# Slots and banks of a hybrid decoder layer handed out as its list scheduler reckoned, by recording the program twice

## The chip, the cores and the metric

One core of one Trainium2 chip runs the whole program. The metric is the device time of one execution in microseconds (us), lower is better. The core has five engines with an instruction queue each: TensorE (PE, matrix products), VectorE (DVE), ScalarE (ACT), GpSimd (POOL), and SyncE (SP), which here only issues DMA transfers. Instructions of one queue start in their order; between queues, semaphores hold an instruction back until its operands and its destination are ready.

## The reference: what is computed

One inference step of one decoder layer, float32, for a prompt of 2048 tokens and a decode group of 8 sequences with one token each, which share the weights. D_MODEL is 1024.

```python
y, conv_buf, sc_buf, s = parallel_mixer(rms_norm(x, norm_mix), ...)   # conv module beside gated DeltaNet, one output projection
x = x + y
x = x + memory_attend(rms_norm(x, norm_mem_q), mem_k, mem_v, w_mq, w_mo)   # 4 heads of 256 into 256 memory tokens
x = x + swiglu(rms_norm(x, norm_ffn), w_gate, w_up, w_down)               # D_FF 2816
```

The mixer projects the normalised input once. One half of the columns goes through a gated linear unit, a depthwise convolution of width 31, a layer norm and SiLU; the other half is a gated DeltaNet (4 heads of 128, chunks of 64, a recurrent 128x128 state). The memory keys and values come from 256 memory tokens. Outputs are the final norms, the conv and delta states, and the memory keys and values.

## The kernel before, in words

The prompt is worked in four blocks of 512 tokens (NB = 4, TB = 512), activations transposed: 128 channels on the partitions, tokens along the free dimension. Blocks go through the mixer in pairs, then output projection, attention and feed-forward block by block. The decode tokens' work is mixed in between. Weights arrive as 128x512 tiles called raw, are split by ScalarE into a rounded part (`w<-raw`) and by VectorE or GpSimd into the remainder (`w<-raw,w`), and TensorE multiplies with both. The feed-forward products and some others are cut further into partial products (fx, fy, fz, dx, dy, dz in the profile), which need sums of weight tiles; those sums are stored in DRAM once (`sums<-w`, `sums<-raw`) and loaded again (`w<-sums`, `raw<-sums`).

The program isn't issued in the order in which it is written. Everything is first recorded on a tape (class `Tape`): each operation with its engine, outputs, inputs and a reckoned cost (`Tape.cost`, lines 189 to 221). `Tape.order` (lines 316 to 522) is a list scheduler: it keeps a reckoned clock for each engine, always takes the engine that can start first, and takes from the operations that are ready there the one with the lowest key. `Tape.issue` then issues the operations in that order to the framework, which adds the semaphores. As every operation has the line of the call in `issue`, the profile shows L530 throughout, and groups are told apart by the names of their tiles.

Tiles live in slots. A pool has for each tag a number of slots of one size; a tile of that tag takes a slot and gives it back after its last reader. The tags that carry most of the work are: `raw` (11 slots, loaded weights), `w` (6 slots, split weights), `t2` (28 slots of 520 floats, nearly all intermediate values, among them the profile's jn, pr, kt, qb, vtd, acc, sqj, lnx), `act` (22 slots, the matmuls' activations) and, in PSUM, `mm` and `s` (three banks each) and `o` and `cv` (one bank each). An operation that begins a tile can't start before the last reader of its slot's tile before has ended, on whatever engine that is.

`Tape.order` reckons with this. For each tag it keeps a heap `free` of the times at which slots come free (line 345). An operation that begins a tile isn't taken while the lowest entry lies in its future (lines 446 and 447); when it is taken, the lowest entry is popped (line 471). When a tile's last operation is placed, its reckoned end goes back into the heap: the end of the operation plus 160 ns, or for a DMA plus 930 ns (lines 514 to 517). A DMA's end is reckoned as its issue plus 1100 ns, or the end of the transfer before if that is later, plus its size at 295 bytes per ns (lines 207 and 498); a GpSimd `tensor_tensor` as 150 ns plus 2.15 ns per element (line 221), a VectorE reduction as 68 ns plus 1.042 ns per element.

What `order` does not say is which slot it was. `TapePool.tile` (lines 550 to 557) asks the framework for a tile of the tag with its number of slots, and the framework picks the slot itself, from what it knows of the issued order.

Of the kernel before, what the change touches and what calls it, by code (L numbers as in the profile page):

```python
# [8 lines left out]
F32 = mybir.dt.float32  # L9
# [71 lines left out]
class Clock:  # L81


    def __init__(self):
        self.at = {"pe": 0.0, "act": 0.0, "dve": 0.0, "pool": 0.0, "sp": 0.0, "dma": 0.0}
        self.ready, self.used = {}, {}
        self.table = None
        self.ring, self.nbank = {}, {"mm": 3, "s": 3, "o": 1, "cv": 1}
        self.held = set()
# [65 lines left out]
class Tape:  # L155
# [8 lines left out]
        "dma": dict(pe=930, dve=950, act=910, pool=985, sp=930),  # L164
    }

    def __init__(self):
        self.ops, self.tag_of, self.bufs, self.psum, self.flex = [], {}, {}, set(), True
        self.real, self.other, self.given, self.follow = {}, {}, {}, set()

    def pool(self, pool, bufs, psum=False):
        return TapePool(self, pool, bufs, psum)
# [143 lines left out]
    def order(self):  # L316
# [15 lines left out]
        line, at, live = {}, {}, {}  # L332
# [9 lines left out]
                heappush(held, last[t])  # L342
                live[tag].append(len(held))
        key = self.keys(succs, line, first, tiles)
        free = {tag: [0.0] * self.bufs[tag] for tag in line}
        head = dict.fromkeys(line, 0)
        early = {tag: set() for tag in line}
        parked = {tag: [] for tag in line}
# [25 lines left out]
        start, end, ends = [0.0] * N, [0.0] * N, {}  # L374
# [8 lines left out]
        def cost(n, e):  # L383
            return self.ops[n][7] if e == self.ops[n][0] else self.other[n][2]
# [17 lines left out]
        done = []  # L402
        while len(done) < N:
            best = None
            for e in engines:
                if avail[e]:
                    t = clock[e]
                elif future[e]:
                    t = max(clock[e], future[e][0][0])
                else:  # L410
                    continue
                if best is None or t < best[0]:
                    best = t, e
            assert best is not None, "order"
            t, e = best
            fu, av = future[e], avail[e]
            while fu and fu[0][0] <= t:
                _, k, n = heappop(fu)
                heappush(av, (k, n))
            skipped = []  # L420
            load = taken(t) if e == "pool" else 0.0
            busy = e != "pool" or load > BACKLOG
            n = None
            while av:
                k, n = heappop(av)
                if gone[n]:
                    n = None
                    continue
                if not busy and n in self.other:
                    load += cost(n, "dve")[0]  # L430
                    busy = load > BACKLOG
                    n = None
                    continue
                at_ = bank_at(n, e)
                if at_ > t:
                    ready[n] = at_
                    heappush(fu, (ready[n], key[n], n))
                    n = None
                    continue
                new = [x for x in tiles[n] if x not in given]  # L440
                stop = None
                for x in new:
                    tag = self.tag_of[x]
                    if not may(x) or not free[tag]:
                        stop = tag, None
                    elif free[tag][0] > t:
                        stop = tag, free[tag][0]
                if stop is None:
                    if e == "dve" and cost(n, e)[1] and port_at > t + 150 and not skipped:

                        other = [(k2, m) for k2, m in av if not gone[m] and not cost(m, e)[1] and all(x in given for x in tiles[m]) and bank_at(m, e) <= t]
                        if other:
                            skipped.append((k, n))
                            k, n = min(other)
                            av.remove((k, n))
                            heapify(av)
                            new = []
                    break
                if stop[1] is None:
                    parked[stop[0]].append((e, n))  # L460
                else:
                    ready[n] = stop[1]
                    heappush(fu, (ready[n], key[n], n))
                n = None
            for x in skipped:
                heappush(av, x)
            if n is None:
                continue
            for x in new:
                tag = self.tag_of[x]  # L470
                heappop(free[tag])
                given.add(x)
                if at[x] == head[tag]:
                    ts = line[tag]
                    while head[tag] < len(ts) and ts[head[tag]] in given:
                        early[tag].discard(head[tag])
                        head[tag] += 1
                else:
                    early[tag].add(at[x])
                if parked[tag]:  # L480
                    wake(tag, t)
            ns, port, tb = cost(n, e)
            gone[n] = True
            self.given[n] = e
            s = t
            if port and e in ("dve", "pool"):
                s = max(s, port_at)
                port_at = s + ns
            if tb and tb != table:
                table = tb  # L490
                ns += 1283
            if e == "pe" and s > clock[e] + 1800 and s > 5000:
                slow = s + 3400
            if e == "pe" and s < slow:
                ns *= 1.9
            if e == "sp":
                clock[e] = s + 450
                dma_at = max(dma_at, s + 1100) + ns
                fin = dma_at
            else:  # L500
                clock[e] = fin = s + ns
            start[n], end[n] = s, fin
            done.append(n)
            for x in banks[n]:
                bank[x] = e, max(fin, bank[x][1]) if x in bank and bank[x][0] == e else fin
            lat = self.LAT["dma" if e == "sp" else e]
            for m in succs[n]:
                left[m] -= 1
                ready[m] = max(ready[m], fin + (max(lat["dve"], lat["pool"]) if m in self.other else lat[self.ops[m][0]]))
                if not left[m]:  # L510
                    push(m)
            for x in tiles[n]:
                uses[x] -= 1
                ends[x] = max(ends.get(x, 0.0), fin + (930 if e == "sp" else 160))
                if not uses[x]:
                    tag = self.tag_of[x]
                    heappush(free[tag], ends[x])
                    early[tag].discard(at[x])
                    if parked[tag]:
                        wake(tag, ends[x])  # L520
        self.start, self.end = start, end
        return done

    def issue(self, tc):
        with tc.manual_schedule():
            for n in self.order():
                eng, _, fn, args, kw, *_ = self.ops[n]
                if self.given[n] != eng:
                    fn = self.other[n][1]
                fn(*args, **kw)  # L530

# [14 lines left out]
class TapePool:  # L546
# [1 line left out]
        self.tape, self.real, self.bufs, self.psum = tape, pool, bufs, psum  # L548

    def tile(self, shape, dt, tag, name, bufs=None):  # L550
        t = self.real.tile(shape, dt, tag=tag, name=name) if bufs is None else self.real.tile(shape, dt, tag=tag, name=name, bufs=bufs)
        tp = self.tape
        key = (id(self), tag)
        tp.tag_of[t.name] = key
        tp.bufs[key] = bufs or self.bufs
        if self.psum:
            tp.psum.add(t.name)
        return t
# [91 lines left out]


@with_exitstack
def hybrid_step(ctx: ExitStack, tc: tile.TileContext, i: dict, o: list):
    nc = tc.nc
    C = Clock()
    tape = Tape()
    tape.real = {"dve": nc.vector, "pool": nc.gpsimd}
    GS, PE, SP = tape.port(nc.gpsimd, "pool"), tape.port(nc.tensor, "pe"), tape.port(nc.sync, "sp")
    V, A, G = Engine(tape.port(nc.vector, "dve"), "dve", C), Engine(tape.port(nc.scalar, "act"), "act", C), Engine(GS, "pool", C)
# [140 lines left out]
    class Plan(list):  # L800


        def __init__(self):
            self.raws, self.raw_of, self.uses, self.seen = [], [], [], []
# [21 lines left out]
    plan = Plan()  # L826
# [146 lines left out]
    for pair in PAIRS:  # L973
        for st in STEPS:
            k = int(st[1])
# [1323 lines left out]
    for pair in PAIRS:  # L2299
# [3 lines left out]
        for st in STEPS:  # L2303
# [8 lines left out]
            k = int(st[1])  # L2312
# [801 lines left out]
    for b in range(NB):  # L3114
# [5 lines left out]
        elif b + 1 < NB:  # L3120
            rest()
    S.until(lambda: not S.lanes, "end")
    tape.issue(tc)


_OUTS = [
    (KC, P, SEQ), (P, KC, DEC), (4, P, CW - 1), (P, 12, SC - 1), (1, 1, H, DK, DK), (1, 1, NM, MH, MD), (1, 1, NM, MH, MD),
    (1, DEC, CW - 2, CC), (1, DEC, SC - 2, QKV), (1, DEC, H, DK, DK), (P, 4, DEC), (P, 12, DEC),
]
# [75 lines left out]
```

## Time and profile before

| what | us |
|---|---|
| median of 3 runs (2897.68 to 2903.99) | 2903.49 |
| the profiled execution's own time | 2902.07 |
| its span, first to last instruction | 2900.4 |
| PE busy | 2851.7 |
| weight loads (PEld) busy | 2574.5 |
| DVE busy | 2456.9 |
| ACT busy | 1519.2 |
| POOL busy | 816.2 |

The span is a little shorter than the time of the execution, which has the start and the end around it. Busy times are of single engines that run beside each other. In rows such as `PE sc <- ACT pr: 4.0, 2, 3.6` the waiting engine and the tile that it writes stand left of the arrow, what ended the wait right of it, then the total in us, the number of waits and the longest. In a timeline row, start and length come first, then engine, operation, output and inputs, and in brackets how long the engine was idle before it and what ended that.

### The profile page before, as it was taken

What the parts mean: (1) busy time and instruction counts of PE and PEld (TensorE: products, weight loads), DVE (VectorE), ACT (ScalarE), POOL (GpSimd) and SP (SyncE); (2) the same over time, 40 slices, a digit from 0 to 9 for tenths busy, and PEclk for the clock granted to TensorE, in tenths of its full rate; (3) what the DMA queues carried; (4) which work ended last, traced back from release to release, by engine and by line L of the source; (5) the groups of instructions that cost most, each with busy time, mean ns of one, the idle gap of its engine ahead of it and who ended that gap; (6) DMA issues with size and microseconds to landing.
All of it is one profiled execution on the core that took longest, in us unless ns stands there. A gap on an engine that the chain in (4) does not pass through costs nothing.

```text
span 2900.4 us, 55620 instructions
## 1 busy us (share of the span) xinstructions
PE 2851.7 (98%) x19240; PEld 2574.5 (89%) x19240; DVE 2456.9 (85%) x5321; ACT 1519.2 (52%) x3426; POOL 816.2 (28%) x969
## 2 busy tenths in 40 slices
PE   9999999999899999999999999999999999999998
PEld 7999878887788787899988789999889999999998
DVE  8868999999777997998989778888867888888888
ACT  7554565646765555556555454444554444444444
POOL 3211333346235015563313710000631232400000
PEclk9999999999999999999999999999999999999999
DMA  6433434778764325766677677777527666676664
GB/s 221 146 112 102 135 123 162 239 256 251 225 217 137 119 95 166 239 200 223 219 259 263 224 247 236 251 238 238 185 89 231 206 211 196 207 238 189 216 211 129
DMA packets 363034, 569.39 MB, mean 196 GB/s; under 512 B 55840, under 2 KB 158560, under 8 KB 362736
## 3 DMA queue, kind: packets, MB, share of 16 engines
q1 hardware_dynamic: 362752, 565.84, 60.9%
q8 instruction: 152, 2.49, 0.4%
q14 instruction: 130, 1.06, 0.1%
HBM read 457.77 MB, written 108.51 MB: 195 GB/s over the span
## 4 chain that ended last, share of the span: by engine, by line
PE 84%; DVE 6%; DMA 4%; ACT 2%; issue 2%; POOL 2%; SPq 0%; DVEq 0%; POOLq 0%; ACTq 0%
PE rg L530 11%; PE fy L530 11%; PE hd L530 10%; PE fz L530 8%; PE fx L530 8%; PE dx L530 5%; PE dn L530 5%; PE sc L530 5%; PE dz L530 3%; PE glub L530 2%; PE glua L530 2%; PE mkv L530 1%; PE pu L530 1%; DVE w L530 1%; PE dy L530 1%
## 5 line engine op out<-in xcount | busy, mean ns | idle before, releaser
L530 ACT ACTIVATE w<-raw 128x512 fp32r<-128x512 f32 (+1 forms) x1066 | 649.2, 619 | 818.5 <-issue 141.0
L530 DVE TENSOR_TENSOR w<-raw,w 128x512 fp32r<-128x512 f32 (+1 forms) x849 | 600.6, 711 | 154.8 <-ACT w L530 150.3
L530 PE MATMUL fy<-op,w 128*128 128x256 f32 (+1 forms) x3168 | 434.4, 283 | 5.8 <-DVE ffs L530 5.8
L530 PEld LDWEIGHTS fy<-op,w 128*128 128x128 f32 x3168 | 400.8, 189 | 9.0 <-DVE ffs L530 6.0
L530 POOL TENSOR_TENSOR w<-raw,w 128x512 fp32r<-128x512 f32 (+1 forms) x217 | 306.8, 1420 | 306.4 <-ACT w L530 202.6
L530 PE MATMUL hd<-hT,w 128*128 128x512 f32 (+2 forms) x1920 | 390.7, 356 | 2.2 <-DVE w L530 1.1
L530 DVE SCALAR_TENSOR_TENSOR cacc<-cu,cw,cacc 128x512 f32<-128x512 f32 x480 | 358.2, 746 | 6.6 <-ACT cacc L530 3.4
L530 PEld LDWEIGHTS hd<-hT,w 128*128 128x128 f32 x1920 | 305.1, 189 | 48.0 <-ACT w L530 2.0
L530 PE MATMUL fx<-op,w 128*128 128x256 f32 (+1 forms) x2112 | 296.7, 283 | 0.1
L530 PE MATMUL fz<-op,w 128*128 128x256 f32 (+1 forms) x2112 | 287.5, 283 | 2.1 <-DMA w<-sums 2.0
L530 PEld LDWEIGHTS fx<-op,w 128*128 128x128 f32 x2112 | 269.2, 188 | 6.3 <-issue 2.6
L530 PEld LDWEIGHTS fz<-op,w 128*128 128x128 f32 x2112 | 264.2, 188 | 8.4 <-DMA w<-sums 3.3
L530 PE MATMUL dx<-fo,w 128*128 128x256 f32 (+1 forms) x1344 | 199.0, 283 | 1.6 <-DVE x L530 1.6
L530 PE MATMUL sc<-w,hT 128*128 128x512 f32 x768 | 190.6, 402 | 4.0 <-ACT pr L530 4.0
L530 PE MATMUL rg<-pT,w 128*128 128x512 f32 x768 | 191.1, 401 | 3.0 <-ACT pT L530 1.4
L530 PE MATMUL dn<-ff,w 128*128 128x512 f32 (+2 forms) x960 | 191.9, 353 | 0.4 <-DVE ffs L530 0.4
L530 PE MATMUL rg<-catS,w 128*128 128x512 f32 (+2 forms) x960 | 191.5, 354 | 0.0
L530 PEld LDWEIGHTS dx<-fo,w 128*128 128x128 f32 x1344 | 174.9, 188 | 5.3 <-DVE x L530 3.8
L530 PEld LDWEIGHTS rg<-catS,w 128*128 128x128 f32 x960 | 155.9, 189 | 24.1
L530 PEld LDWEIGHTS sc<-w,hT 128*128 128x128 f32 x768 | 142.0, 189 | 37.4 <-ACT pr L530 6.0
L530 PEld LDWEIGHTS rg<-pT,w 128*128 128x128 f32 x768 | 141.9, 189 | 36.5 <-ACT pr L530 2.2
L530 PEld LDWEIGHTS dn<-ff,w 128*128 128x128 f32 x960 | 151.9, 189 | 23.1 <-DVE x L530 0.9
(435 smaller groups left out, 4898.0 us busy)
## 6 DMA issues: line engine op xcount, KB each, us to landing
w<-sums SPq DMA_DIRECT2D x222, 512.0 KB, 4.5
raw<-in_w_gate_dram SPq DMA_DIRECT2D x192, 256.0 KB, 3.5
sums<-w SPq DMA_DIRECT2D x66, 512.0 KB, 4.0
raw<-in_w_up_dram SPq DMA_DIRECT2D x118, 256.0 KB, 3.6
raw<-in_w_down_dram SPq DMA_DIRECT2D x224, 128.0 KB, 3.0
raw<-in_w_in_dram SPq DMA_DIRECT2D x96, 256.0 KB, 3.1
raw<-sums SPq DMA_DIRECT2D x74, 256.0 KB, 3.2
raw<-wk SPq DMA_DIRECT2D x64, 256.0 KB, 2.8
```

Source lines behind the costliest of these rows:

```text
L530: fn(*args, **kw)
```

## The change

The program is recorded twice. The first recording runs `order` and returns the tape, which keeps the order (`done`), the engine given to each operation (`given`) and, new, for each tile the number of the slot that `order` popped for it (`place`). The heap's entries become pairs of time and slot number for this. The second recording builds the same program on a fresh context with the first tape as its plan; its `TapePool.tile` looks up the number that the plan holds for the tile that was created at the same place of the recording, and asks the framework for a tile of a tag of its own for that slot (`mm_0`, `mm_1`, `t2_17`) with one slot. So the framework has no choice left. It issues the operations in the plan's order on the plan's engines; both are what `order` gave before, since the pairs are popped by their time. Tags with one slot, DRAM tiles among them, stay as they are.

```diff
-        free = {tag: [0.0] * self.bufs[tag] for tag in line}
+        free = {tag: [(0.0, k) for k in range(self.bufs[tag])] for tag in line}
...
-                    elif free[tag][0] > t:
-                        stop = tag, free[tag][0]
+                    elif free[tag][0][0] > t:
+                        stop = tag, free[tag][0][0]
...
-                heappop(free[tag])
+                self.place[x] = heappop(free[tag])[1]
...
-                    heappush(free[tag], ends[x])
+                    heappush(free[tag], (ends[x], self.place[x]))
...
-        self.start, self.end = start, end
+        self.start, self.end, self.done = start, end, done
...
     def issue(self, tc):
         with tc.manual_schedule():
-            for n in self.order():
+            for n in self.plan.done:
                 eng, _, fn, args, kw, *_ = self.ops[n]
-                if self.given[n] != eng:
+                if self.plan.given[n] != eng:
                     fn = self.other[n][1]
                 fn(*args, **kw)
...
     def tile(self, shape, dt, tag, name, bufs=None):
-        t = self.real.tile(shape, dt, tag=tag, name=name) if bufs is None else self.real.tile(shape, dt, tag=tag, name=name, bufs=bufs)
+        plan = self.tape.plan
+        if plan and (bufs or self.bufs) > 1:
+            t = self.real.tile(shape, dt, tag=f"{tag}_{plan.place[plan.names[len(self.tape.names)]]}", name=name, bufs=1)
+        elif bufs is None:
+            t = self.real.tile(shape, dt, tag=tag, name=name)
+        else:
+            t = self.real.tile(shape, dt, tag=tag, name=name, bufs=bufs)
         tp = self.tape
+        tp.names.append(t.name)
...
-def hybrid_step(ctx: ExitStack, tc: tile.TileContext, i: dict, o: list):
+def hybrid_step(ctx: ExitStack, tc: tile.TileContext, i: dict, o: list, slots=None):
...
-    tape = Tape()
+    tape = Tape(slots)
...
+    if slots is None:
+        tape.order()
+        return tape
     tape.issue(tc)
...
+    nc, ins, outs = program()
+    plan = hybrid_step(_tile.TileContext(nc).__enter__(), ins, outs)
+    nc, ins, outs = program()
     with _tile.TileContext(nc) as tc:
-        hybrid_step(tc, ins, outs)
+        hybrid_step(tc, ins, outs, plan)
```

More of the change, by code (lines that the diff above doesn't have):

```diff
@@ L165, with __init__ @@
     }
-    def __init__(self):
+    def __init__(self, plan=None):
         self.ops, self.tag_of, self.bufs, self.psum, self.flex = [], {}, {}, set(), True
         self.real, self.other, self.given, self.follow = {}, {}, {}, set()
+        self.place, self.names, self.plan = {}, [], plan
     def pool(self, pool, bufs, psum=False):
@@ L3192, with program @@
     from concourse.bass_utils import run_bass_kernel_spmd as _run
-    nc = _bacc.Bacc("TRN2", target_bir_lowering=False, num_devices=1, dynamic_dma_scratch_size=1024)
-    arrays, ins, outs = {}, {}, []
-    for name, a in lay_out(inputs).items():
-        arrays[f"in_{name}_dram"] = a
-        ins[name] = nc.dram_tensor(f"in_{name}_dram", a.shape, _mybir.dt.from_np(a.dtype), kind="ExternalInput").ap()
-    for k, shape in enumerate(_OUTS):
-        outs.append(nc.dram_tensor(f"out_{k}_dram", shape, F32, kind="ExternalOutput").ap())
+    arrays = {f"in_{name}_dram": a for name, a in lay_out(inputs).items()}
+    def program():
+        nc = _bacc.Bacc("TRN2", target_bir_lowering=False, num_devices=1, dynamic_dma_scratch_size=1024)
+        ins, outs = {}, []
+        for name, a in arrays.items():
+            ins[name[3:-5]] = nc.dram_tensor(name, a.shape, _mybir.dt.from_np(a.dtype), kind="ExternalInput").ap()
+        for k, shape in enumerate(_OUTS):
+            outs.append(nc.dram_tensor(f"out_{k}_dram", shape, F32, kind="ExternalOutput").ap())
+        return nc, ins, outs
+    nc, ins, outs = program()
+    plan = hybrid_step(_tile.TileContext(nc).__enter__(), ins, outs)
+    nc, ins, outs = program()
     with _tile.TileContext(nc) as tc:
-        hybrid_step(tc, ins, outs)
+        hybrid_step(tc, ins, outs, plan)
     r = _run(nc, [arrays], core_ids=[0])
```

## The prediction

> **What bounds the kernel now.** I began with the page's totals.
>
> ```profile
> span 2900.4 us, 55620 instructions
> ...
> PE 2851.7 (98%) x19240; PEld 2574.5 (89%) x19240; DVE 2456.9 (85%) x5321; ACT 1519.2 (52%) x3426; POOL 816.2 (28%) x969
> ...
> PE 84%; DVE 6%; DMA 4%; ACT 2%; issue 2%; POOL 2%; SPq 0%; DVEq 0%; POOLq 0%; ACTq 0%
> ```
>
> TensorE is busy for all but 2900.4 - 2851.7 = 48.7 us, and the chain that ended last (third line) runs through it for 84%. The change adds and removes no matmul, and it issues each queue in the same order as before; it only decides which slot a tile lies in. So it can win back no more than part of these 48.7 us, and what a lower clock costs behind them. Next I read what TensorE waited for, in the view of waits of that engine.
>
> ```profile
> PE fy L530 <- DVE ffs L530: 5.8, 1, 5.8
> PE sc L530 <- ACT pr L530: 4.0, 2, 3.6
> PE wk L530 <- ACT jn L530: 3.0, 2, 1.7
> PE pu L530 <- DMA Tm<-zt: 2.0, 1, 2.0
> PE fz L530 <- DMA w<-sums: 2.0, 4, 0.9
> ...
> PE rg L530 <- ACT pT L530: 1.4, 2, 1.1
> PE po L530 <- ACT osc L530: 1.4, 1, 1.4
> ...
> PE hd L530 <- ACT w L530: 1.1, 1, 1.1
> ```
>
> Few waits are long, and each happens once or twice. The longest, 5.8 us, is of a matmul whose second half goes into a bank from which VectorE still has to read the first half; VectorE came late to that read because of its own queue. No slot is part of it. In the next two the bank of the matmul is waited for, and ScalarE, which empties it, is late. Whether ScalarE was late because of a slot is the question, so I looked at the timeline and the chain around both.
>
> ```profile
> 1643.12 7.96 POOL L530 TENSOR_TENSOR kt<-kt,qb 128x512 f32<-128x512 f32 x6
> ...
> 1646.14 0.68 DVE L530 TENSOR_REDUCE scs<-kt 128x2 f32<-128x512 f32 x1
> ...
> 1649.89 0.56 ACT L530 ACTIVATE pr<-sc,mx,rs 128x256 f32<-128x256 f32 x1 [4.24 <-POOL kt L530]
> ...
> 1651.15 1.97 PE L530 MATMUL sc<-w,hT 128*128 128x512 f32 x6 [3.55 <-ACT pr L530]
> ```
>
> Here is the mechanism that the change is about. `pr` reads sc, mx and rs. It reads nothing that GpSimd wrote, yet ScalarE stood idle for 4.24 us until a GpSimd product ended. So the new pr tile was given the t2 slot of a qb tile that GpSimd was still reading. At 1646.14 + 0.68 = 1646.82 VectorE had finished its last read of a kt tile, three microseconds sooner; the slot of that one went to another tile. GpSimd's product had its place earlier in the order, and ended later.
>
> ```profile
> 754.93 5.70 DMA wk<-jn
> ...
> 760.66 0.70 ACT jn L530
> ...
> 761.40 0.79 PE wk L530 x2
> ```
>
> The chain around the other wait shows a slot too: jn is written from PSUM, and had to wait for the DMA that still stored the jn tile before it in that slot.
>
> **The change, part by part.** The forecast is made against the profiled execution, 2902.07 us with a span of 2900.4; the median of the three runs, 2903.49, lies 1.42 above it.
>
> *Slots that GpSimd reads last (pr).* The scheduler reckons a GpSimd product over 512 elements at 150 + 512 x 2.15 = 1251 ns, and 160 ns until the slot is free: 1.41 us. It reckons VectorE's reduction at 68 + 512 x 1.042 = 602 ns, free after 0.76 us. With both started within 0.65 us of each other VectorE's slot is free first by its reckoning, and pr gets that one. I take it so, as GpSimd's slot was the oldest by order alone. Then pr begins at about 1646.84, its two activations and their accumulator reads take about 1.2 us, and the matmul that began at 1651.15 begins at 1648.1. But the pr tile after it is in the same position.
>
> ```profile
> 1649.82 1.26 POOL L530 TENSOR_TENSOR kt<-kt,qb 128x512 f32<-128x512 f32 x1
> ...
> 1651.11 0.56 ACT L530 ACTIVATE pr<-sc,mx,rs 128x256 f32<-128x256 f32 x1
> ```
>
> GpSimd ended the next product at 1651.08, and the next pr began at 1651.11. If that tile keeps its slot, its bank comes free at about 1651.11 + 1.2 = 1652.3 as before; TensorE has done the six matmuls of the row of 1651.15 by 1648.1 + 1.97 = 1650.1 and waits there for 2.2 us. Before, it had done them at 1653.1; now it goes on at 1652.3: 0.8 us won of a wait of 3.55. That is what is late next. The ends are 0 (pr keeps its slot) and 3.0 us (all of them get other slots).
>
> The clock comes on top. The windows view gives the granted clock around both waits.
>
> ```profile
> 759.50:761.40 1.90, 0.21 (x3) 0.02 (x2) 1.32 (x3) 0.74 (x2) 0.00 (x0) 1.00 0.01 2
> 761.40:764.90 3.50, 3.50 (x16) 3.50 (x17) 0.00 (x0) 1.90 (x6) 0.00 (x0) 0.51 0.77 263
> ...
> 1652.30:1655.80 3.50, 3.50 (x11) 2.58 (x10) 3.21 (x10) 1.11 (x5) 0.00 (x0) 0.51 0.03 5
> ```
>
> The first number behind the window's length is TensorE's busy time, the third from the end the clock. After each of the two idle stretches the clock is halved for 3.5 us, which costs half of that, 1.7 us. With pr's wait broken into pieces of 0.5 and 2.2 us the halving may stay away or not; a stretch with 0.21 us busy in 1.90 was enough at 761, so I count half, 0.85 us. Sum of this part: 0.8 + 0.85, about 1.7 us won; bounds 0 and 3.0 + 1.7 = 4.7.
>
> [...]
>
> pr's old slot now goes to another taker, most likely a load of vtd, which was issued in those microseconds. SP then waits for GpSimd, up to 3.0 us, with the loads queued behind it. I cost that at nothing, as TensorE waits for weight loads so rarely (below); without that cover it is the 3.0 us.
>
> *Slots that a DMA reads last (jn, stored w).* The store of jn took 5.70 us. Reckoned it is 1.10 + 262144 / 295 = 0.89 + 0.93 = 2.92 us. Both the framework and the plan took or take this slot for free when it isn't; I see no reason for another choice and cost it at 0. Its bounds are the waits of 3.0 us with the halved clock, 1.7, won; and on the other side new waits of this kind. The nearest rows for those:
>
> ```profile
> sums<-w SPq DMA_DIRECT2D x66, 512.0 KB, 4.0
> ACT w L530 <- DMA sums<-w: 12.7, 9, 4.7
> L530 ACT ACTIVATE w<-raw 128x512 fp32r<-128x512 f32 (+1 forms) x1066 | 649.2, 619 | 818.5 <-issue 141.0
> ```
>
> A stored w tile takes 4.0 us and is reckoned at the same 2.92, so its slot seems free 1.1 us too soon; nine of these 66 already hold ScalarE up, by 1.4 us each. ScalarE has room (818.5 us idle before `w<-raw`), and of that only 1.1 us reached TensorE (`PE hd <- ACT w`). Upper end: 5 us lost, as if one wait like pr's came back with its clock.
>
> *Slots of raw tiles and SP's queue.* A raw tile is last read by ScalarE, VectorE or GpSimd.
>
> ```profile
> SPq L530 <- POOL w L530: 253.4, 147, 11.3
> L530 DVE TENSOR_TENSOR w<-raw,w 128x512 fp32r<-128x512 f32 (+1 forms) x849 | 600.6, 711 | 154.8 <-ACT w L530 150.3
> L530 POOL TENSOR_TENSOR w<-raw,w 128x512 fp32r<-128x512 f32 (+1 forms) x217 | 306.8, 1420 | 306.4 <-ACT w L530 202.6
> ```
>
> GpSimd's product takes 1.42 us, VectorE's 0.71. Where GpSimd's slot was taken first only because it was placed first, the load behind it starts up to 0.7 us sooner, 147 times at most. TensorE waited for DMAs for 2.0 + 2.0 us in its view, and no raw load is among them, so the bounds are 4.0 us won and nothing. I take 0.5, near the low end, since eleven raw slots lie between load and use.
>
> *PSUM banks.* TensorE writes the banks in order, and with three in turn the one freed longest ago is the same by the order of issue and by reckoned ends, unless two readers overtake each other. `rg <- pT` and `po <- osc` (1.4 us each) are such waits; o has one bank and no choice. I take 0, with 1.4 us either way. Further waits on other semaphores than before are a few instructions each and lie beside TensorE's work.
>
> Sum: 1.7 + 0 + 0.5 + 0 = 2.2 us won. 2902.07 - 2.2 = 2899.9 for the profiled execution, and 2903.49 - 2.2 = 2901.3 for the median.
>
> **Rivals.**
>
> *Nothing changes.* The framework may choose almost as the plan does, so that only a handful of tiles lie elsewhere, pr among those that don't move. For it: the list above holds only one TensorE wait that another choice would clearly have spared. It gives 2903.5. Chance 0.2, within "same".
>
> *Faster.* Every slot wait falls: pr 4.7, the two waits for jn and the clock 3.0 + 1.7 = 4.7, DMA 4.0, one bank 1.4, together 14.8: 2888.7; half of it, 7.4 us, gives 2896.1. For it: one trace shows pr and jn by their names, and smaller ones may hide behind other releasers. Against: jn's slot was reckoned free, and TensorE takes back little where the next tile is late as well. Chance 0.25.
>
> *Slower: GpSimd later than reckoned.* The plan trusts GpSimd to free a slot 1.41 us after the start of the product. At 1643 it had six products queued back to back (7.96 us), and the last ended eight microseconds after the first began. Where GpSimd lags behind its reckoned start by more than the slack of the slot, the plan hands ScalarE or VectorE the later slot with confidence. Each such place on the way to a bank costs what pr's did, 3.55 + 1.7 = 5.25 us. It decides from two new places on: 2 x 5.25 - 2.2 = 8.3 us lost, 2911.8. Against: GpSimd is busy for only 28%, and by order alone it was preferred even more. Chance 0.13.
>
> **How the numbers follow.** What a measurement can tell from no change is about 0.2%, 5.8 us. The forecast of 2.2 us won has 0.42 and lies within it, as does "nothing changes" with 0.2: 0.62 for the same. Faster has 0.25, slower 0.13. The likeliest case alone spans 2898 to 2904. The range for all cases reaches down to 2893, which takes in the nearer half of the faster rival, and up to 2909, short of the slower one at its two places but with a single one.
>
> **What would show it.** Right: TensorE's count stays at 19240, its idle time falls to about 46 us, `ACT pr <- POOL kt` of 4.24 us near 1650 shrinks to about 1, a wait of sc on pr of some 2 us remains, SP waits less than 253.4 us for POOL w, and wk's waits for jn stay at 3.0. Wrong: an unmoved pr (nothing changes); both jn and pr gone and an idle time under 40 us (faster); new waits of TensorE above 3 us behind ScalarE with a GpSimd releaser, each followed by half a clock (slower).

## The result, and the profile after

The kernel after the change takes 2893.48 us (median of 20 executions, 2890.08 to 2901.0), the kernel before beside it 2901.62 (20 executions, 2895.35 to 2906.7). The ratio is 0.9977, 95% interval 0.9969 to 0.9985: 6.7 us faster, 4.4 to 9.0. Two more comparisons (e6 and e11 below) gave 9.9 and 8.7 us. The forecast was 2.2 us and "the same" within 0.2%; the ratio lies just beyond that bound, and the time inside the range of 2893 to 2909, by half a microsecond. One execution of e9 below took 3068.63 us, far above all others, and is left out of its median and ratio.

The two profiled executions show less of it, 2902.07 us against 2899.17. The latter is one of the slowest of its 20 executions; part of why executions of one kernel differ by several us is in the last section. First the totals of the page after the change.

```profile
span 2897.4 us, 55611 instructions
...
PE 2849.6 (98%) x19240; PEld 2574.3 (89%) x19240; DVE 2460.6 (85%) x5321; ACT 1520.3 (52%) x3426; POOL 813.4 (28%) x969
```

TensorE's count is the same. Its idle time went from 48.7 us to 2897.4 - 2849.6 = 47.8. So busy and idle totals hardly tell the kernels apart. What does is the view of TensorE's waits (after the change; line 531 stands where 530 stood before).

```profile
PE fy L531 <- DVE ffs L531: 5.8, 1, 5.8
PE fz L531 <- DMA w<-sums: 2.3, 4, 1.1
PE wk L531 <- ACT jn L531: 2.1, 3, 1.3
PE hd L531 <- DVE w L531: 2.1, 1, 2.1
...
PE vp L531 <- ACT jn L531: 1.9, 3, 0.9
...
PE sc L531 <- ACT pr L531: 1.1, 1, 1.1
```

`sc <- pr` fell from 4.0 us in two waits to 1.1 in one. The waits for jn changed their form (wk 3.0 to 2.1, vp 0.6 to 1.9), not their sum (3.6 and 4.0). The timeline around pr, after the change:

```profile
1644.76 8.05 POOL L531 TENSOR_TENSOR kt<-kt,qb 128x512 f32<-128x512 f32 x6
1645.99 1.26 DVE L531 TENSOR_REDUCE scs<-kt 128x2 f32<-128x512 f32 x2
1646.70 0.56 ACT L531 ACTIVATE pr<-sc,mx,rs 128x256 f32<-128x256 f32 x1 [1.97 <-DVE scs L531]
...
1647.95 3.45 PE L531 MATMUL sc<-w,hT 128*128 128x512 f32 x13 [1.07 <-ACT pr L531]
...
1648.49 0.57 ACT L531 ACTIVATE pr<-sc,mx,rs 128x256 f32<-128x256 f32 x1 [0.58 <-DVE scs L531]
...
1651.10 0.57 ACT L531 ACTIVATE pr<-sc,mx,rs 128x256 f32<-128x256 f32 x1 [1.40 <-DVE scs L531]
```

GpSimd's six products are as long as before (8.05 us, 7.96 before), but none of these pr waits for them: all three are released by VectorE's reductions. The slot of every tile in the two programs says the same: pr_3565, pr_3566 and pr_3567 (the three activations with a wait) each had a qb tile's slot, which GpSimd reads, and now have a kt tile's, which VectorE reads. The row at 1649.89 in the prediction is the second of the three, pr_3566. The first, in the timeline of before:

```profile
1644.45 0.56 ACT L530 ACTIVATE pr<-sc,mx,rs 128x256 f32<-128x256 f32 x1 [1.36 <-POOL kt L530]
...
1645.70 1.89 PE L530 MATMUL sc<-w,hT 128*128 128x512 f32 x7 [0.45 <-ACT pr L530]
```

So the wait of 1.07 us that is left after the change stands at pr_3565, where it was 0.45 before: there the new slot came free later than the old one. The wait of 3.55 us at pr_3566 is gone, and at pr_3567 TensorE doesn't wait. The windows view has the clock of the stretch that was at 0.51 before:

```profile
1652.30:1655.80 3.50, 3.50 (x18) 2.83 (x17) 3.50 (x8) 2.98 (x7) 2.03 (x3) 1.00 0.02 5
```

18 matmuls instead of 11 in the same 3.5 us, at the full clock.

There is a second place, which the longest waits of the list don't show. Timeline of before, then of after:

```profile
516.46 0.72 ACT L530 ACTIVATE acc<-raw,scw 128x512 f32<-128x512 f32 x1 [1.59 <-PE pu L530]
...
517.20 0.55 ACT L530 ACTIVATE u<-pu 64x128 f32<-64x128 f32 x2
...
517.81 0.49 PE L530 MATMUL pch<-S,kT 128*128 128x128 f32 x2 [0.64 <-ACT u L530]
```

```profile
515.50 0.73 ACT L531 ACTIVATE acc<-raw,scw 128x512 f32<-128x512 f32 x1 [1.06 <-DMA q<-acc]
...
517.09 0.56 ACT L531 ACTIVATE u<-pu 64x128 f32<-64x128 f32 x2 [0.86 <-PE pu L531]
```

The tile acc_1028 had the slot of lt_753, which TensorE's pu matmul still had to read: ScalarE, which makes acc, waited for TensorE, and `u`, queued behind acc, then held TensorE up. Now it has the slot of acc_1015, which a DMA was storing, and the store landed first. The same run of instructions, from one `po` matmul to one `hd` matmul, in the windows view of before and of after:

```profile
512.66:524.89 12.23, 11.23 (x61) 8.70 (x60) 10.74 (x23) 6.01 (x16) 4.35 (x6) 1.00 0.59 190
```

```profile
513.30:523.98 10.68, 10.68 (x62) 8.81 (x60) 9.48 (x21) 4.83 (x13) 3.53 (x5) 1.00 0.51 165
```

12.23 us became 10.68, and TensorE's 1.00 us without work is gone.

Two more of TensorE's waits are smaller still. Timeline of before, then of after:

```profile
480.24 0.63 PE L530 MATMUL pu<-W,u 128*128 128x64 f32 x4 [0.82 <-DVE zd L530]
...
891.57 0.66 PE L530 MATMUL pvv<-ident,vT 128*128 128x128 f32 x4 [0.33 <-DVE tbm L530]
```

```profile
480.91 0.63 PE L531 MATMUL pu<-W,u 128*128 128x64 f32 x4
...
893.56 0.60 PE L531 MATMUL pvv<-ident,vT 128*128 128x128 f32 x4
```

The matmuls are the same and the waits are gone. For pvv the slots name the reason: in its bank lay a dnc tile that VectorE still had to read (into tbm), and now lies a pu tile that ScalarE reads sooner. For pu the tile in its bank is the same as before, and VectorE has read it by the time TensorE gets there; which moved slot does that isn't traced.

In all, the order on every engine is the same, and of the 3889 tiles of the tags t2, raw, w and s that have a tile before them in their slot, 363 lie behind another one than before (234 of t2, 80 raw, 29 s, 20 w); none of mm and act does.

### The profile page after: what moved, and what is told of

Read it like the earlier page. It is cut to its first block, busy times and chain, and to the rows that moved or that the text cites. A ratio compares the mean times of both kernels' runs of the same rounds, so it can differ in the third digit from the quotient of the medians.

```text
span 2897.4 us, 55611 instructions
## 1 busy us (share of the span) xinstructions
PE 2849.6 (98%) x19240; PEld 2574.3 (89%) x19240; DVE 2460.6 (85%) x5321; ACT 1520.3 (52%) x3426; POOL 813.4 (28%) x969
## 4 chain that ended last, share of the span: by engine, by line
PE 85%; DVE 6%; DMA 4%; ACT 2%; issue 2%; POOL 1%; SPq 0%; DVEq 0%; ACTq 0%; POOLq 0%
PE rg L531 12%; PE fy L531 11%; PE hd L531 11%; PE fx L531 7%; PE fz L531 7%; PE dn L531 6%; PE sc L531 5%; PE dx L531 5%; PE glub L531 3%; PE dz L531 3%; PE glua L531 3%; DMA w<-sums 2%; PE pu L531 1%; DVE w L531 1%; PE pch L531 1%
## 5 line engine op out<-in xcount | busy, mean ns | idle before, releaser
L531 PEld LDWEIGHTS hd<-hT,w 128*128 128x128 f32 x1920 | 306.1, 190 | 48.7 <-DVE w L531 2.6
```

## The experiments

The first theory was that the gain is made at pr, with the clock behind it; e2 made it **theory 1** of the later runs: it is made at two places, pr and acc. **Rivals:** it is the 230 other t2 tiles, or the raw, w and PSUM slots with SP's queue, or the naming of slots by itself. Every kernel was compared with the kernel before on the same chip; us are the ratio's distance from 1 times the median of before. The slots of a kernel are changed by a table of slot numbers or by `trade(x, y)`: from tile x on, the slot of x and the slot of y are exchanged in the plan, for all later tiles.

**e1, pr alone.** The slots of before by table, and

```diff
+        for x, y in [('pr_3565', 'kt_3592'), ('pr_3566', 'kt_3599'), ('pr_3567', 'kt_3608')]:
+            tape.trade(x, y)
```

> The slots of before, written out as a table, and only three pr tiles (and the tiles that trade places with them) moved to the slots that they have after the change. Theory A (one place): the change won its time at the pr tiles near 1650 us, where the two profiles differ by 4 to 5 us (TensorE's waits of 3.55 and 0.45 us and a halved clock worth 1.7 us). Then this kernel takes 4 to 5 us less than before, about 2897, and most of what the change won (6.7 us by the ratio 0.9977). Theory B (many places): the 363 tiles of 3889 that lie elsewhere win a little each, and pr is one of them by accident of this one profile; then this kernel is within 2 us of before.

Measured: 2896.78 us against 2901.12, ratio 0.9984 (0.9974 to 0.9993), 4.6 us faster (2.0 to 7.5). Its timeline has pr as in the kernel after:

```profile
1642.67 0.56 ACT L547 ACTIVATE pr<-sc,mx,rs 128x256 f32<-128x256 f32 x1 [1.97 <-DVE scs L547]
...
1643.92 3.45 PE L547 MATMUL sc<-w,hT 128*128 128x512 f32 x13 [1.07 <-ACT pr L547]
```

Three tiles, with their partners in the trades, give about half of what the kernel after won in its three comparisons, as theory A had it.

**e2, pr undone.** The kernel after, with the three pr tiles back behind qb tiles.

```diff
+        for x, y in [('pr_3565', 'qb_3597'), ('pr_3566', 'qb_3602'), ('pr_3567', 'qb_3607')]:
+            tape.trade(x, y)
```

> The changed kernel with only those three pr tiles put back behind the GpSimd products, the other moved tiles as changed. Theory A: 4 to 5 us slower than the changed kernel, so within 3 us of before (2 us faster than it at most), with TensorE's wait of 3.5 us for pr and the halved clock near 1652 back in the profile. Theory B: it keeps nearly all of the gain, 5 to 7 us faster than before.

Measured: 2896.35 us against 2901.12, ratio 0.9982 (0.9973 to 0.9991), still 5.2 us faster (2.6 to 7.8). The wait is back in its view (the first row), but most of the gain isn't gone with it. That pr is the whole of it was wrong; something else in the plan earns time. Its timeline led to the second place, where acc is released by the DMA as in the kernel after:

```profile
PE sc L539 <- ACT pr L539: 4.0, 2, 3.5
```

```profile
516.77 0.72 ACT L539 ACTIVATE acc<-raw,scw 128x512 f32<-128x512 f32 x1 [1.97 <-DMA q<-acc]
```

**e3, the plan's slots for t2 only, and e7, for all other tags only.**

```diff
-        if plan and (bufs or self.bufs) > 1:
+        if plan and (bufs or self.bufs) > 1 and tag in ('t2',):   # e7: ('raw', 'w', 's', 'mm', 'act')
```

> The plan's slots for the tag t2 alone; raw, w, PSUM banks and the small tags are left to the framework's own choice. If the gain lies in t2 (234 moved tiles, pr among them), it is 5 to 7 us faster than before like the changed kernel. Rival: the raw slots and SyncE's queue (80 moved tiles of raw) carry a part; then 2 to 4 us of the gain are missing here.

> The plan's slots for raw, w and the PSUM banks alone (129 moved tiles), t2 left to the framework. If only pr and its neighbours in t2 count, it is within 2 us of before. If the undone pr tiles left 4 us of gain because of these tags, it is 3 to 5 us faster than before.

Measured: e3 2897.72 us against 2901.12, ratio 0.9985 (0.9975 to 0.9995), 4.4 us faster (1.5 to 7.3), which lies between its two forecasts and holds both; e7 2902.43 against 2903.62, ratio 0.9996 (0.9986 to 1.0006), within the measurement of no change (1.2 us, -1.7 to 4.1). SP's waits in e7 and, below, in the kernel before:

```profile
SPq L531 <- DVE w L531: 631.7, 374, 9.7
SPq L531 <- POOL w L531: 229.8, 143, 11.3
```

```profile
SPq L530 <- DVE w L530: 610.8, 358, 9.6
```

SP waited 24 us less for GpSimd (253.4 before) and 21 us more for VectorE. The loads wait for the other reader instead, and no time that can be measured comes of it.

**e5, the slots of before, handed out by number** (the control: the table, with no trade).

> A control: the slots of before, all of them, but handed out through the new way (a table, one tag for each slot). If only the choice of slots counts, it is within 1.5 us of before. Rival: naming each slot (other addresses in SBUF, another set of waits) is itself worth something; then it is 2 to 4 us faster than before, and that share has to be taken off every gain measured so far.

Measured: 2902.04 us against 2903.62, ratio 0.9996 (0.9985 to 1.0007). The naming of slots costs and brings nothing that shows.

**e4, slots by the measured ends.** A table from a plan that pops the slot whose last reader ended first in the profile of the kernel after, DMA landings included, in place of the reckoned ends.

> Same order, but each slot is chosen as the one whose last reader ended first in the profile of the changed kernel, DMA landings included, instead of by reckoned ends. If choosing by true ends matters beyond pr, the waits of TensorE for jn (2.1 us for wk, 1.9 us for vp, and the halved clock at 763, 1.7 us) shrink, and it is 3 to 6 us faster than the changed kernel, 9 to 13 us faster than before. Rival: at these places hardly any slot is free, so that choice is spent; then it is within 2 us of the changed kernel.

Measured: 2896.71 us against 2901.12, ratio 0.9980 (0.9970 to 0.9990), 5.8 us faster than before and no better than the kernel after. Knowing the ends of one execution exactly, the DMA's too, isn't worth more that these executions could show. This table leaves pr_3565 behind the qb tile of before and moves the other two, and its stretch at pr is as short as that of the kernel after (14.46 us, table below): the move of pr_3565 is worth nothing.

**e6 and e11, the kernel after the change again,** beside e5 and e7, and beside e8 to e10.

> The changed kernel itself, beside the control on one chip, with a second profile of it. Expected 5 to 8 us faster than before, as measured. The second profile tells how much of a profile is chance: theory A says that the stretch at the pr tiles looks as in the first (a wait of about 1 us, no halved clock behind it), while the halved stretches elsewhere fall in other places.

> The kernel after the change beside the three above: its earlier medians were 6.7 and 9.9 us (ratios 0.9977 and 0.9966) better than before, so 0.9965 to 0.998 is expected by every theory; it sets what the others are compared with.

Measured: 2891.84 us against 2903.62, ratio 0.9966 (0.9954 to 0.9977), and 2892.62 against 2902.31, ratio 0.9970 (0.9959 to 0.9981).

**e8, both places undone.** The kernel after, with the trades of e2 and

```diff
+        ('acc_1028', 'lt_753'), ('pch_1040', 'pu1_1038')
```

(pch_1040 is the PSUM tile beside it, whose bank the plan had changed too.)

> The kernel after the change, with the slots of before for the three pr tiles, for acc_1028 (the slot of lt_753 again) and for its neighbour pch_1040 (the bank of pu1_1038 again); with the tiles that trade with them, 8 t2 tiles and 2 PSUM tiles differ from the kernel after. Theory 1, the gain is made at these two places (4.6 us at pr with the clock, 1.7 us at acc): within 2 us of the kernel before, ratio 0.9993 to 1.0007. Theory 2, the other two hundred t2 tiles earn a part of it, as the run with pr alone undone kept 5 us: 3 to 5 us faster than before, ratio below 0.999.

Measured: 2901.41 us against 2902.31, ratio 0.9999 (0.9988 to 1.0010). Ten tiles differ from the kernel after, the three pr tiles, acc_1028 and pch_1040 among them back behind their tiles of before, and no gain is left that can be told from 0 (0.3 us, -2.9 to 3.5), though 226 t2 tiles, 80 raw, 27 s and 20 w tiles still lie as the plan wants them. Both waits are back in its timeline:

```profile
517.97 0.72 ACT L539 ACTIVATE acc<-raw,scw 128x512 f32<-128x512 f32 x1 [2.65 <-PE pu L539]
```

```profile
1654.23 1.67 PE L539 MATMUL sc<-w,hT 128*128 128x512 f32 x6 [3.56 <-ACT pr L539]
```

**e12, acc undone alone** (the kernel after with the last two trades only).

> The kernel after the change with the slots of before for acc_1028 (the slot of lt_753, which TensorE reads last) and for pch_1040 (the bank of pu1_1038) alone; 2 t2 tiles and 2 PSUM tiles differ from the kernel after. It is the fourth corner of a square: after measured 6.7 to 9.9 us faster than before, with pr undone 5.2 us, with both undone 0.3 us. Theory 1, the place at 515 is worth what its stretch shows, 1.7 to 1.9 us: 5 to 7 us faster than before, ratio 0.9976 to 0.9983. Theory 2, it is worth the 5 us that lie between the run with pr undone and the run with both undone: 2 to 4 us faster than before, ratio 0.9986 to 0.9993.

Measured: 2895.71 us against 2902.44, ratio 0.9978 (0.9965 to 0.9991), 6.4 us faster (2.6 to 10.2). That is theory 1's figure, but the interval takes in most of theory 2's 2 to 4 us as well. What speaks against 5 us at acc is its stretch, 12.95 us here and 10.68 in the kernel after.

**e9, both places alone.** The slots of before by table, with the trades of e1 and

```diff
+        ('acc_1028', 'acc_1015'), ('pch_1040', 'pch_1008')
```

> The kernel before's slots for every tile but these: the three pr tiles, acc_1028 (the slot of acc_1015) and pch_1040 (the bank of pch_1008), with their partners. Theory 1: 6 to 8 us faster than before, as the kernel after, ratio 0.997 to 0.998, with the stretches at 1643 to 1663 and at 512 to 525 as short as in the kernel after. Theory 2: 4 to 5 us, ratio 0.9983 to 0.9986, as with pr alone.

Measured: 2897.68 us against 2902.31, ratio 0.9987 (0.9976 to 0.9999), 3.8 us faster (0.3 to 7.0): less than theory 1 wanted (6 to 8), with an interval that holds both theories. Its timeline has both places as in the kernel after:

```profile
513.90 0.72 ACT L547 ACTIVATE acc<-raw,scw 128x512 f32<-128x512 f32 x1 [0.85 <-DMA q<-acc]
```

```profile
1644.36 3.45 PE L547 MATMUL sc<-w,hT 128*128 128x512 f32 x13 [1.07 <-ACT pr L547]
```

**e10, a free slot for jn.** The kernel after with one trade, which gives jn_1552 a slot that no DMA holds:

```diff
+        for x, y in [('jn_1552', 'lt_1283')]:
+            tape.trade(x, y)
```

> The kernel after the change with one trade: jn_1552, which got the slot whose jn tile a DMA was still storing, gets the slot of lt_1283, free for long, and jn_1570 gets the other. That DMA waits of jn reach TensorE: the waits of wk for jn (1.3 to 3.0 us) shrink by 1 us or more, and the kernel is 1 to 3 us faster than the kernel after, so 0.9964 to 0.9975 against the kernel before. Rival, the next jn tile waits for the next slot in its place: the waits move to later jn tiles and the time stays within 1 us of the kernel after.

Measured: 2893.44 us against 2902.31, ratio 0.9971 (0.9960 to 0.9983); the kernel after in the same comparison 2892.62. In the waits of its profile `wk <- jn` is no longer there, and this stands:

```profile
PE mkv L539 <- ACT kv L539: 1.8, 1, 1.8
...
PE vp L539 <- ACT jn L539: 0.9, 1, 0.9
```

In e11, the kernel after in the same comparison, the rows are:

```profile
PE wk L531 <- ACT jn L531: 2.4, 2, 1.3
...
PE vp L531 <- ACT jn L531: 0.9, 1, 0.9
...
PE mkv L531 <- ACT kv L531: 0.6, 1, 0.6
```

The waits for jn went, 2.4 us in all, and the median didn't move. Only the second, of 1.1 us, stands at jn_1552; the first, of 1.3 us, is ahead of it, and the `mkv` wait some 60 us ahead. There the two programs are the same, so both belong to the execution and not to the trade. The rival, waits that move to later jn tiles, isn't seen either. Where the 1.1 us went the medians of 7 executions don't tell; the expected 1 to 3 us were not shown, and no version here beats the kernel after beyond its interval.

**The places in all 14 profiles.** The time between the same two TensorE instructions, us, with the half of any halved stretch taken off:

| stretch | with the new slots | with the slots of before |
|---|---|---|
| acc: `po` at 512.7 to `hd` at 524.9 of before | 10.68 to 11.53 (8 kernels), mean 10.92 | 12.23 to 13.16 (6 kernels), mean 12.87 |
| pr: `sc` at 1643.7 to `sc` at 1662.7 | 14.44 to 14.48 (9 kernels) | 17.34 to 17.53 (5 kernels) |
| pu: `hd` at 478.6 to `hd` at 491.0 | 11.52 to 12.07 (9 kernels), mean 11.69 | 12.35 to 12.42 (5 kernels), mean 12.38 |
| pvv: `pu` at 888.4 to `sc` at 894.4 | 5.45 to 5.47 (9 kernels) | 5.98 to 6.00 (5 kernels) |

The groups don't touch, whatever the other slots are. For acc and pr they go by the t2 slots of these tiles (e4 has two of the three at pr), for pu and pvv by the slots of raw, w and s: e1, e3, e5, e9 and the kernel before have the old ones there. At acc the PSUM bank of pch_1040, which was traded with it, isn't the cause: e3 has acc's new slot and leaves the banks to the framework, and its stretch is short (10.99); e7 has the plan's banks and acc's old slot, and its stretch is long (12.93).

acc is worth 1.95 us; pr 2.9, and with the halved clock 4/5 x 1.7 = 1.4 more: 4.3. Of the five kernels with the slots of before four had it behind that wait (before, e2, e5, e7); in after, e1, e3, e9, e10, e11 and e12 the nine sc matmuls that follow took 2.33 to 2.36 us, against 3.11 in the kernel before. The sum of the two is 6.2 us. pu and pvv add 0.7 and 0.5, and two stretches of the same kind (at 235 and at 604) 0.1 each: 1.4 us, in all 7.6. These four were looked for in the profiles after all runs, and no run was made to test them. By the places that each kernel has, e1 should win 4.3 us, e2 3.4, e3 6.2, e7 and e8 1.4, e9 6.2 and e12 5.7. Measured are 4.6, 5.2, 4.4, 1.2, 0.3, 3.8 and 6.4, and each interval holds its sum.

## Why the prediction was right and wrong

*The bound* was right: what was won are waits of TensorE and the clock behind them, far less than the 48.7 us, and the order of every engine stayed.

*pr* was the right place and mechanism, and the main term was mis-sized: 1.7 us forecast, 4.3 shown. The step that failed is "If that tile keeps its slot, its bank comes free at about 1652.3 as before". The rule that moved pr_3566, VectorE's slot reckoned free before GpSimd's, held for pr_3567 as well, so that the wait of 2.2 us expected there is 0; the 1.07 us left over are those of pr_3565, which the prediction didn't look at. The clock, counted at half, then stayed up: it reads 1.00 from 1652.30 to 1655.80 after the change and 0.51 before. The sum of the upper bounds given there, 4.7, was nearly the answer. One reading there is wrong: GpSimd's product was not placed earlier. In the order of issue it stands behind pr_3566 itself, and VectorE's read of the kt tile ahead of it, so "the oldest by order" can't be why the framework chose it; its reason stays open.

A load of vtd took one of the pr tiles' old slots, pr_3565's, as forecast; TensorE's waits have no row that comes of it.

*Slots that a DMA reads last* were put at 0 because both ways "took or take this slot for free when it isn't; I see no reason for another choice". For jn that held: jn_1552 lies in the same slot, and the waits for jn add up to about the same. For acc it failed: there the framework's choice was a slot that TensorE still had to read, and the plan, which reckoned the store's slot free before that one, took the slot with the store under way. So acc began 515.50 - 513.30 = 2.2 us into the stretch and not 516.46 - 512.66 = 3.8, and with `u` and what follows it that won 1.95 us. A reckoned end that is wrong in size still chose rightly between two slots.

*Raw slots and SP* were put at 0.5 us won: e7 shows 1.2 us, -1.7 to 4.1, for these and the banks together, which can't be told from 0, from 0.5 or from the upper bound of 4.0. The forecast that SP would wait less than 253.4 us for GpSimd was right, and meant nothing, since VectorE took over the wait. *PSUM banks* at 0 were not quite right: two readers did overtake each other at pvv, and its stretch is 0.5 us shorter in all nine kernels with the plan's banks, too little for the medians.

*The rivals.* The size is the faster rival's (2888.7 to 2896.1), and its reason half right: more slot waits fell than one, and one was hidden behind another releaser, TensorE itself. Its jn and DMA terms weren't it, and of its 1.4 us for a bank pvv shows 0.5. The slower rival's mechanism is there in small: in the kernel after ScalarE waits 1.8 us in two for GpSimd before it writes acc (`ACT acc <- POOL sqj`), which the kernel before doesn't, and pr_3565's new slot came free 0.6 us later than the old one, with VectorE the late reader. The first doesn't reach TensorE, the second is the 1.07 us above. Of the signs, the idle time of about 46 us was a poor one: it read 47.8 while the medians fell by more than forecast, since a halved stretch counts as busy (3.50 of 3.50 us at a clock of 0.51 from 1652.30 in the kernel before) and other waits differ from one execution to the next. The wait of some 2 us of sc on pr and the 3.0 us of wk for jn, also given as signs, read 1.1 and 2.1.

That the time lies inside the range is luck: the forecast for the median was 2901.3, the first median stands half a microsecond inside the lower end, and those of e6 and e11, 2891.84 and 2892.62, lie below it.

What stays open: the kernel after won 6.7, 9.9 and 8.7 us, mean 8.4, and the places give 7.6. The rest is less than these medians of 7 to 20 executions can tell, and they don't tell either whether e3 and e9, which have acc and pr and not the other places, fall short of 6.2 us (4.4 and 3.8) by more than chance.

## What to carry to other kernels

When a wait's releaser is an engine whose result the instruction doesn't read, ask for the slot: who read the tile before, and did another slot of the tag come free sooner? Follow the choice through all tiles of the burst, since a rule that moves the first moves the next, and cost the wait left over with the moved ones. A slot that a DMA, GpSimd or TensorE reads last is neither good nor bad by its kind; what counts is which ends first, and a rough reckoning of the ends, made once for every tile, found both places that mattered most. It chose wrongly at pr_3565 and at jn, which cost nothing that shows, and the measured ends won nothing more.

## What the runs showed of the clock

Executions of one kernel differ by some 10 us, and a part of that is that TensorE's clock is halved in different stretches: of the 25 of the kernel before beside e8 to e11, the 7 at a granted clock of 0.994 took 2902.9 us in the mean, the 9 at 0.996 took 2899.2. It isn't all: the profiled executions of the kernel after and of e6 are 8.8 us apart, and the granted clock is 0.995 in both. In the records of the kernels before and after the halved stretches, but for the one at the program's end, are 3.41 or 6.83 us long, and within each of the two executions they start a whole number of 3.413 us apart. Before: 761.4, 788.7 (8 steps on), 870.7 (24 more), 945.8 (22), 1194.9 (73), 1652.3 (134). After: 671.5, 763.6 (27), 872.8 (32), 947.9 (22), 1197.1 (73). Divided into such steps, the two records have 8 at full clock with 0 to 1.49 us of TensorE work, and each was followed by half a clock; of 15 with 1.89 to 2.33 us, 3 were; of 1645 with 2.39 us or more, none (the program's end left out). So in these records it is TensorE's work within a step that goes with the clock, not the length of a wait. The windows view shows it for the same wait of pr, 3.6 us, in two kernels with the slots of before there. e5, where the halved stretch begins at 1647.1:

```profile
1643.70:1647.10 3.40, 0.34 (x2) 0.30 (x3) 1.02 (x3) 1.57 (x5) 2.99 (x3) 1.00 0.23 75
1647.10:1650.50 3.40, 3.40 (x11) 2.52 (x10) 3.34 (x9) 1.92 (x8) 0.00 (x0) 0.51 0.00 0
```

and e8, in windows of the same length, the first two of which share the wait:

```profile
1649.10:1652.50 3.40, 1.57 (x7) 0.94 (x5) 2.72 (x5) 0.00 (x0) 3.40 (x3) 1.00 0.72 217
1652.50:1655.90 3.40, 1.67 (x8) 1.35 (x9) 1.69 (x6) 2.72 (x9) 1.66 (x2) 1.00 0.04 14
1655.90:1659.30 3.40, 3.40 (x18) 2.73 (x18) 2.69 (x7) 2.06 (x6) 0.52 (x1) 1.00 0.02 5
```

11 matmuls at half clock there, 18 at full clock here, after the same wait. It works the other way too. In the kernel before two pieces of idle time that end in waits of 1.34 and 1.24 us fell into one step, with 1.41 us of work, and the edge of the next, and the clock halved:

```profile
785.29:788.70 3.41, 1.41 (x11) 1.03 (x10) 2.21 (x4) 3.34 (x6) 1.58 (x4) 1.00 0.87 257
788.70:792.11 3.41, 2.82 (x8) 2.25 (x9) 1.75 (x4) 3.35 (x6) 0.00 (x0) 0.51 0.93 314
```

So a wait of 3.56 us left the clock full in e8, and two of 1.34 and 1.24 in the kernel before did not. Without the stretch at the program's end the profiles of before and after have 27.3 and 23.9 us of halved time, worth half of that, 13.7 and 11.9 us. The stretches differ from one execution to the next (e6, the same kernel as after, is at full clock from 761.4 to 764.9, where after is halved from 763.6), and a change that wins less has to be read from its own stretch of the trace, with the halved time taken off, or from many executions.
